# A matmul kernel with a planned order: one stored pair fewer, a finer table of bandwidth shares in the planner, and another layout of the scratch tiles in DRAM

## The chip, the cores and the metric

One core of one Trainium2 chip runs one launch of the kernel. The time is the device time of that launch in microseconds (us); smaller is better. The kernel before was run three times; the median counts.

## The reference

```python
def reference(a, b, bias):          # a, b: 4096 x 4096 float32, bias: 4096
    return np.tanh(np.matmul(a, b) + bias)
```

## The kernel before

**Two levels of Strassen.** The kernel computes the product in fp16 (all loads from `a` and `b` cast from float32 on their way in) with fewer multiplications than the plain method. Rows go in *pairs* of 2 x 128 rows, sixteen in all (`NP`), and two pairs form a *duo* (eight duos). Columns go in four blocks of 1024 (`c` = 0 to 3). For a pair, A is a 2 x 2 matrix of tiles: a11, a12, a21, a22, each 128 rows by 2048 of the inner dimension, 4 KB per partition in fp16. The seven products P1 to P7 need four of these or their sums s1 to s4. At the second level (`fine_left`, `fine_right`, `Fine`) two pairs together are split once more: a product of two pairs is made from seven products of half tiles with 256 columns instead of eight. So most matmuls of the program are 128x256 (line 798), the rest 128x512 (lines 783 and 1560).

**The stages.** *The opening* (lines 1456 to 1663) computes column block 0 for the row blocks 0 to 7, which are the pairs 0 to 3, with plain matmuls while the first data arrives. Then, still for c = 0, `run_duo` takes the duos 2 to 7 in turn. Their A is read from the input in natural order (`natural_tile`, line 504: four DMAs by 32 partitions on POOL's queue, and two DVE transposes, line 476, per tile of 1 MB of float32), the sums are formed on DVE, and the four tiles a11, a12, a22, s2 (`BASIS`) of each pair are written to DRAM scratch (`keep`, line 550), so that the later column blocks can fetch them without a transpose. For c = 1, 2, 3 the kernel runs `pass_one` (products P1 and P2, and P6 for c = 2, 3) over all duos, and `pass_two` (P7, P6, P5, P4, P3) over all duos in reverse order. B's block of 1024 columns is read raw for each c (`raw_b`, line 717: sixteen tiles of 1 MB on POOL's queue); its sums are formed on DVE.

**What is stored, and when.** `FIRST = (0,)` (line 42) makes pair 0, one of the four pairs of the opening, a stored pair: at the end of the opening, lines 1656 to 1660 form s1 and s2 of pair 0 on DVE and write a11, a12, a22, s2 (512 KB each) to scratch on SP's queue. Pairs 1, 2 and 3 aren't stored; when c = 1 first needs them, `upper` (line 1229) reads a11 and a12 from the input once more, by natural tiles, and stores them, and later, in `pass_two`, `others` (line 1239) does so for a21 and a22, forms the sums and stores a22, s2 and s1, s3, s4. For a stored pair these two functions only fetch from scratch. With `ORDER[1] = (7, 6, 5, 0, 4, 1, 3, 2)` duo 0 (pairs 0 and 1) is the fourth duo of `pass_one` for c = 1, and the fifth of `pass_two`.

**The scratch in DRAM.** Each name of each duo has one DRAM tile of five half tiles (line 421, `[P, 5, TP, P]`; a half tile is 2 KB per partition, 256 KB in all). All five halves of a partition lie side by side, so a partition's row is 10 KB, and a transfer of two neighbouring halves (`move`, line 538, on SP's queue) is 128 pieces of 4 KB; a transfer of one half is 128 pieces of 2 KB. The traffic with scratch is most of what SP's queue carries; the rest of it are the output tiles (256 KB each, pieces of 2 KB), the partial sums `state` (512 KB, pieces of 4 KB) and the bias.

**What sets the order.** No order is written out by hand across engines. All work is recorded as operations with an engine, an estimated duration, an emitter, reads and writes (`Plan.add`, line 150), ranked by due time (`rank`), and placed by a list scheduler (`schedule`, line 218) that plays the program through with its own durations. The order in which it starts the operations is the order of the instructions on each engine; nothing else of it reaches the chip. Two DMA queues are played: POOL's (all loads from `a` and `b`) and SP's (everything else), each with at most `RING = 8` DMAs under way. When both carry something, `rates` (line 277) deals the bandwidth: SP's transfer gets 0.64 if it is a load into SBUF and 0.47 if it is a store (`SHARE`, line 51), POOL gets the rest. A load is only placed when a buffer of the 51 `PLACES` is free.

Of the kernel before, what the change touches and what calls it, by code (L numbers as in the profile page):

```python
# [10 lines left out]
P = 128  # L11
# [6 lines left out]
TP = T // 2  # L18
# [3 lines left out]
fp16 = mybir.dt.float16  # L22
# [16 lines left out]
THREE = (False, False, True, True)  # L39
LATER = 6  # L40
HOLD = (1, 1, 1, 1)
FIRST = (0,)
WHOLE = ()
SPARE = ("a11", "a12", "a22")
AHEAD = (("s1", "s3", "s4"), ("s1", "s3", "s4"), ("s1", "s3", "s4"), ("s1", "s3", "s4"), (), ())
# [2 lines left out]
SMALL = 5  # L48
RING = 8
DMA = {"POOL": (384e3, 3.65), "LATER": (384e3, 5.0), "in": (399e3, 3.86), "out": (369e3, 3.5)}  # L50
SHARE = (0.64, 0.47)
RISE = ((), (4, 4, 4, 4, 4, 4, 4, 4), (4, 4, 4, 4, 4, 4, 4, 4), (4, 4, 4, 4, 4, 4, 4, 4))
SECONDS = (0, 8, 8, 8)
STEEP = ((0, 1, 1, 1, 1, 2), (), ())
# [73 lines left out]
class Op:  # L128
    __slots__ = (
        "parts", "n", "eng", "dur", "lag", "emit", "preds", "succs", "bufs", "nbytes", "hw", "soft", "early", "lead", "reach", "far",  # L130
        "unsent", "flying", "flow", "wait",
        "due", "left", "start", "done", "ready",
    )

# [1 line left out]
class Plan:  # L136
# [10 lines left out]
        self.bufs.append(buf)  # L147
        return buf

    def add(self, eng, dur, emit, reads=(), writes=(), nbytes=0, hw=True, soft=None, early=0.0, lead=0.0, reach=1e9, after=None):  # L150
        early, far = early if isinstance(early, tuple) else (early, self.FAR)
        op = Op()
        op.n, op.eng, op.dur, op.emit = len(self.ops), eng, dur, emit
        op.nbytes, op.hw, op.soft, op.early, op.lead = nbytes, hw, soft, early, lead
        op.parts = 4 if dur > 1 and not hw else 1
        op.reach, op.far = reach, far
        if nbytes:
            kind = "LATER" if not hw and early else "POOL" if not hw else "out" if soft is not None else "in"
            op.flow, op.wait = nbytes / DMA[kind][0], DMA[kind][1]
        op.lag = op.wait + op.flow if nbytes else self.LATE  # L160
        preds, seen = set(), {}
        for group, writing in ((reads, False), (writes, True)):
            for access in group:
                buf, atoms = access if isinstance(access, tuple) else (access, access.atoms)
                if isinstance(buf, Bank):
                    if eng == "PE":
                        preds |= buf.rest
                        buf.rest = set()
                        buf.pe = op
                        buf.writer, buf.readers = {}, {}  # L170
                        continue
                    if buf.pe:
                        preds.add(buf.pe)
                    buf.rest.add(op)
                else:
                    seen[buf] = True
                for i in atoms:
                    if i in buf.writer:
                        preds.add(buf.writer[i])
                    if writing:  # L180
                        preds.update(buf.readers.get(i, ()))
                        buf.writer[i], buf.readers[i] = op, []
                    else:
                        buf.readers.setdefault(i, []).append(op)
        if after:
            preds.add(after)
        preds.discard(op)
        op.bufs = [b for b in seen if b.cls]
        for b in op.bufs:
            b.users += 1  # L190
        if eng == "PE":
            if self.last_pe:
                preds.add(self.last_pe)
            self.last_pe = op
        op.preds = preds
        op.succs = []
        for p in sorted(preds, key=lambda p: p.n):
            p.succs.append(op)
        self.ops.append(op)
        return op  # L200
# [17 lines left out]
    def schedule(self):  # L218
# [9 lines left out]
        pipes = {e: [] for e in ready}  # L228
# [47 lines left out]

        def rates():

            live = [(e, p) for e, p in pipes.items() if p]
            if len(live) == 1:  # L280
                return [(live[0][1], 1.0)]
            part = {p[0][1].eng: SHARE[p[0][1].soft is not None or not p[0][1].bufs] for _, p in live if p[0][1].hw}
            return [(p, 1 - sum(part.values()) if e == "POOL" else part[e]) for e, p in live]

        def flow(now):
            shares = rates() if any(pipes.values()) else []
            for p, r in shares:
                p[0][0] -= (now - clock[0]) * r
            clock[0] = now
            ended = False  # L290
            for p, _ in shares:
                while p and p[0][0] < 1e-6:
                    op = p.pop(0)[1]
                    op.done = now + op.wait
                    heapq.heappush(events, (op.done, op.n, 1))
                    ended = True
            return ended

        def next_flow(now):
            if any(pipes.values()):  # L300
                clock[1] += 1
                at = now + min(max(p[0][0], 1e-6) / r for p, r in rates())
                heapq.heappush(events, (at, clock[1], 3))

        while events:
            now = events[0][0]
            while events and events[0][0] <= now + 1e-9:
                _, n, kind = heapq.heappop(events)
# [3 lines left out]
                elif kind == 4:  # L312
                    op = self.ops[n]
# [3 lines left out]
                elif kind == 1:  # L317
                    op = self.ops[n]
# [16 lines left out]
                elif kind == 2:  # L335
                    op = self.ops[n]
                    insort(ready[op.eng], (op.due, op.n))
            for eng, waiting in ready.items():
# [5 lines left out]
                for i, (_, n) in enumerate(waiting):  # L344
                    op = self.ops[n]
# [34 lines left out]
def kernel(  # L380
# [18 lines left out]
    dram = ctx.enter_context(tc.tile_pool(name="dram", bufs=1, space=bass.MemoryType.DRAM))  # L399
    ctx.enter_context(tc.manual_schedule())  # L400

    plan = Plan()
    add, new = plan.add, plan.buf

    def fixed(name, shape, dtype):
# [12 lines left out]
    for i in range(NP // 2):  # L418
        for name in STORED:
            buf = scratch[name, i] = Buf(f"{name}_{i}", None, cls=None, atoms=5)  # L420
            buf.tile = dram.tile([P, 5, TP, P], fp16, name=f"{name}_{i}")

    states = []
    for i in range(NP // 2):
        buf = Buf(f"state_{i}", None, cls=None)
# [11 lines left out]
    def dve(n, emit, reads, writes, wide=False, **kw):  # L437
        add("DVE", 0.08 + n / (960 if wide else 1900), emit, reads, writes, **kw)

    def act(n, emit, reads, writes, **kw):  # L440
        add("ACT", 0.09 + n / 1200, emit, reads, writes, **kw)
# [11 lines left out]
    ALL = slice(None)  # L453
# [8 lines left out]
    def finish(src, row, col):  # L462

        o = new("o", [P, NB], fp32, "out")
        act(NB, lambda: nc.scalar.activation(o[ALL], src[ALL], TANH), (src,), (o,), soft=2.0)
        store(o, row, col, NB)
# [27 lines left out]
    def load_rows(tl, srcs, nbytes):  # L494


        def emit():
            for q in Q_ORDER:
                src, key = srcs(q)
                nc.gpsimd.dma_start(out=tl[(ds(q * QP, QP), *key)], in_=src)  # L500

        add("POOL", 4 * 0.55, emit, (), (tl,), nbytes=nbytes, hw=False)

    def natural_tile(pair, name, s, soft=None):

        r, h = int(name[1]) - 1, int(name[2]) - 1
        tl = new("nat", [P, 4, T * QP])
        s[name] = new(name, [P, T, P], atoms=2)

        def srcs(q):  # L510
            src = a[ds((2 * pair + r) * P, P), ds(q * KQ + h * T * QP, T * QP)]
            return src.rearrange("(mb p) k -> p mb k", p=QP), ()

        load_rows(tl, srcs, P * T * P * 4)
        for u in range(2):

            def emit(dst=s[name], tl=tl, u=u):
                transpose(dst, tl[ALL, ds(2 * u, 2), ALL], 0, u * 2 * QP)

            add("DVE", turn_time(1024), emit, (tl,), ((s[name], (u,)),), soft=soft)  # L520
# [17 lines left out]
    def move(name, duo, first, tl, t0, n, out, **kw):  # L538

        box = scratch[name, duo]  # L540
        dram_, key = (box, range(first, first + n)), (ALL, ds(t0 * TP, n * TP))
        sb = tl if out else (tl, range(t0, t0 + n))

        def emit():
            far, near = box[ALL, ds(first, n)], tl[key].rearrange("p (n t) m -> p n t m", n=n)
            nc.sync.dma_start(out=far if out else near, in_=near if out else far)

        add("SP", 0.34, emit, (sb if out else dram_,), (dram_ if out else sb,), nbytes=P * n * TP * P * 2, **kw)
# [906 lines left out]

    early = set(range(4, NP)) | set(FIRST)

# [9 lines left out]
    def mb(m, j):  # L1467
        return banks[2 * (m % 4) + j]
# [14 lines left out]
    first = new("first", [P, 4, 4, TB * QP], atoms=4)  # L1483
# [169 lines left out]
    for m, j in swapped:  # L1653
        down(m, j, T, 2 * T, stop=True)
        finish(mb(m, j), m, j * NB)
    for p in FIRST:
        s = {f"a{r + 1}{h + 1}": aq[2 * p + r, h] for r in range(2) for h in range(2)}
# [114 lines left out]
```

## Time and profile before

| | |
|---|---|
| median of 3 runs | 1464.31 us (1462.56 to 1467.89) |
| the profiled execution | 1466.24 us, of which 1464.5 us are the span from first to last instruction |
| mean granted TensorE clock | 0.997 |
| busy in the span | PE 1444.2 us, DVE 1112.8, ACT 461.3, POOL 304.3 |
| SP's DMA queue (q1) | 318.29 MB, 62.1% of the 16 DMA engines' span |
| POOL's DMA queue (q0) | 73.44 MB written, 31.4% |
| HBM, read and written | 324.01 MB and 141.03 MB |

PE is the matmul engine, DVE the vector engine, ACT the scalar engine, POOL the engine that issues the loads from the inputs, SP the one that issues all other DMAs. A row of the grouped views has: line, engine, operation, out<-in, count, then busy time and mean duration of one. A row of the timeline has: start, duration, engine, line, operation, count, and in brackets how long the engine sat idle before it and who ended that wait. A row of the DMA view has: queue, packets, MB, share of the 16 engines' time in the stretch asked for; MB of q0 are counted as written, after the cast, which is half of what is read. A queue's packets are the pieces of its transfers and, for about one in nine, a semaphore write of 4 bytes.

### The profile page before, as it was taken

The page shows a single profiled execution, that of the slowest core. Times are in us where ns is not written, and L with a number is a line of the kernel's source. Part 1 is how long each engine was busy: PE and PEld are TensorE (multiplying, and loading weights), DVE is VectorE, ACT ScalarE, POOL GpSimd, SP SyncE. Part 2 cuts the span into 40 slices and gives each one's busy share as a digit, 9 for nine tenths or more (in the row PEclk, how much of TensorE's full clock was granted, in tenths as well). Part 3 has the DMA queues.
Part 4 walks back from the last instruction along what each step waited for, and adds up shares of the span by engine and source line. Part 5 has one row for each costly group of instructions (what it writes and reads, how often), then busy time and mean ns, then how long its engine had stood idle before and what let it go on. Part 6 is the DMA issues. An engine that isn't in the chain of part 4 may idle for free.

```text
span 1464.5 us, 28902 instructions
## 1 busy us (share of the span) xinstructions
PE 1444.2 (99%) x11256; PEld 1101.4 (75%) x11256; DVE 1112.8 (76%) x1739; ACT 461.3 (31%) x1062; POOL 304.3 (21%) x565
## 2 busy tenths in 40 slices
PE   9998999999999999999999999999999999999998
PEld 4444445554578887778878888888888888888887
DVE  3558877776967997785697799977679588986765
ACT  2111111121233332433333332334343332243433
POOL 8754334324333201100130300000210220000000
PEclk9999999999999999999999999999999999999999
DMA  9999999999999979977999988688999897777772
GB/s 175 198 244 293 268 273 288 307 279 272 250 302 316 297 236 281 334 264 287 307 296 348 284 258 288 228 267 272 259 307 340 220 264 267 243 262 270 250 267 89
DMA packets 199754, 393.58 MB, mean 269 GB/s; under 512 B 26048, under 2 KB 92096, under 8 KB 199616
## 3 DMA queue, kind: packets, MB, share of 16 engines
q1 hardware_dynamic: 116928, 318.29, 62.1%
q0 software_dynamic: 82688, 73.44, 31.4%
q8 instruction: 88, 1.44, 0.4%
q14 instruction: 50, 0.41, 0.1%
HBM read 324.01 MB, written 141.03 MB: 318 GB/s over the span
## 4 chain that ended last, share of the span: by engine, by line
PE 74%; DMA 11%; DVE 3%; issue 1%; POOL 1%; ACT 0%; SPq 0%; DVEq 0%; POOLq 0%
PE ps L798 57%; PE ps L783 18%; DMA b<-in_b_dram 6%; DMA nat<-in_a_dram 3%; DMA a<-a 1%; DVE parts L444 1%; DMA bias<-in_bias_dram 0%; DMA out_dram<-parts 0%; DVE ps L444 0%; DVE zs L636 0%; POOL nat L500 0%; DMA out_dram<-p 0%; DMA ys<-s 0%; DVE a L476 0%; DVE s L444 0%
## 5 line engine op out<-in xcount | busy, mean ns | idle before, releaser
L710 POOL DMA_DIRECT2D b<-in_b_dram x256 | 137.6, 541 | 576.9 <-DMA out_dram<-st 197.4
L447 ACT COPY ps<-ps 128x256 f32<-128x256 f32 (+1 forms) x290 | 106.1, 366 | 351.0 <-PE ps L798 334.8
L500 POOL DMA_DIRECT2D nat<-in_a_dram x240 | 129.6, 543 | 300.5 <-DMA nat<-in_a_dram 78.9
L798 PEld LDWEIGHTS <-zs 128*128 128x128 f16 x1424 | 139.3, 98 | 18.6 <-issue 0.7
L798 PEld LDWEIGHTS <-ys 128*128 128x128 f16 x1360 | 133.1, 98 | 15.4
L783 PEld LDWEIGHTS <-s 128*128 128x128 f16 x752 | 74.2, 99 | 90.2 <-issue 8.9
L798 PEld LDWEIGHTS <-ya 128*128 128x128 f16 x1296 | 126.8, 98 | 16.0
L798 PEld LDWEIGHTS <-za 128*128 128x128 f16 x1232 | 120.5, 98 | 14.2 <-issue 0.2
L798 PEld LDWEIGHTS <-xs 128*128 128x128 f16 x1184 | 115.8, 98 | 17.8 <-issue 2.2
L447 ACT COPY parts<-ps 128x256 f32<-128x256 f32 (+1 forms) x185 | 71.6, 388 | 182.9 <-DVE ps L444 83.5
L783 PE MATMUL ps<-t,s 128*128 128x512 f16 x528 | 121.1, 385 | 4.5 <-DVE ps L444 4.5
L798 PEld LDWEIGHTS <-parts 128*128 128x128 f16 x1104 | 108.0, 98 | 12.5
L476 DVE STREAM_TRANSPOSE a<-nat 128x512 uint32<-128x512 uint32 x120 | 78.7, 691 | 50.2 <-DMA nat<-in_a_dram 39.2
L1560 PE MATMUL ps<-b,o 128*128 128x512 f16 x512 | 111.4, 379 | 0.7 <-DVE ps L1585 0.6
L444 DVE TENSOR_TENSOR parts<-ps,parts 128x256 f32<-128x256 f32 (+1 forms) x173 | 75.9, 439 | 47.4 <-PE ps L798 39.3
L798 PEld LDWEIGHTS <-xa 128*128 128x128 f16 x1024 | 100.2, 98 | 14.6 <-issue 2.7
L783 PEld LDWEIGHTS <-a 128*128 128x128 f16 x592 | 57.9, 98 | 67.7
L444 DVE TENSOR_TENSOR ps<-ps,parts 128x256 f32<-128x256 f32 (+1 forms) x189 | 83.8, 445 | 24.6 <-PE ps L798 15.7
L636 DVE TENSOR_TENSOR zs<-xs,ys 128x2048 f16<-128x2048 f16 x74 | 90.1, 1218 | 15.4 <-PE ps L798 11.5
L798 PE MATMUL ps<-b,zs 128*128 128x256 f16 x784 | 101.6, 273 | 0.0
L1560 PEld LDWEIGHTS <-o 128*128 128x128 f16 x512 | 49.8, 98 | 60.9 <-issue 1.0
L636 DVE TENSOR_TENSOR za<-xa,ya 128x2048 f16<-128x2048 f16 x60 | 73.1, 1218 | 17.0 <-DMA out_dram<-cs 10.5
(140 smaller groups left out, 2533.9 us busy)
## 6 DMA issues: line engine op xcount, KB each, us to landing
ys<-s SPq DMA_DIRECT2D x74, 512.0 KB, 5.0
xs<-s SPq DMA_DIRECT2D x74, 512.0 KB, 5.3
b<-in_b_dram POOLq DMA_DIRECT2D x256, 128.0 KB, 8.5
ya<-a SPq DMA_DIRECT2D x64, 512.0 KB, 6.4
xa<-a SPq DMA_DIRECT2D x64, 512.0 KB, 6.7
nat<-in_a_dram POOLq DMA_DIRECT2D x240, 128.0 KB, 9.1
out_dram<-parts SPq DMA_DIRECT2D x112, 256.0 KB, 6.1
a<-a SPq DMA_DIRECT2D x32, 512.0 KB, 7.5
```

The costliest lines, as they stand in the source:

```text
L444: dve(n, lambda: nc.vector.tensor_tensor(out=o(), in0=x(), in1=y(), op=op), reads, writes, wide, **kw)
L447: act(n, lambda: nc.scalar.copy(o(), x()), reads, writes, **kw)
L476: nc.vector.transpose(dst[ALL].rearrange("P t m -> P (t m)").bitcast(pair32).rearrange("P (U m) -> P U m", m=P)[:, ds(t0 // 2, nu), ds(row ...
L500: nc.gpsimd.dma_start(out=tl[(ds(q * QP, QP), *key)], in_=src)
L636: nc.vector.tensor_tensor(out=halves(z), in0=halves(x), in1=halves(y)[:, ds(0, 1)].broadcast_to([P, 2, TP * P]), op=SUB,)
L710: nc.gpsimd.dma_start(out=dst.rearrange("p t j n -> p t (j n)") if j is None else dst, in_=src)
L783: nc.tensor.matmul(bank[ALL], left_tile(left, k + t + shift), rb.tile(t), start=start and k == t0 and t == 0, stop=k + t == t0 + nt - 1, s ...
L798: nc.tensor.matmul(bank[ALL, HALF[half]], left_tile(buf, at_ * TP + i * TB + t), rb.tile(t), start=False, stop=i == 1 and t == TB - 1, ski ...
L1560: nc.tensor.matmul(bank[ALL], left_tile(left, t), rb.tile(tb), start=start, stop=stop, skip_group_check=True,)
```

## The change

Three edits. `FIRST` becomes empty: no pair of the opening is stored, and pair 0 is treated as pairs 1 to 3 are. The scratch tile becomes `[5, P, TP, P]`: each half tile is one block of 256 KB, with 2 KB per partition, and a transfer of two halves is 256 pieces of 2 KB. The planner's two shares become a table of 2 x 3, which deals POOL's share by what the two queues carry at their heads: POOL's B tiles (0) or A tiles (1), against SP's loads (0), stores to the output (1) or stores to scratch (2).

```diff
-FIRST = (0,)
+FIRST = ()
...
-SHARE = (0.64, 0.47)
+SHARE = ((0.35, 0.51, 0.53), (0.44, 0.47, 0.15))
...
-    def add(self, eng, dur, emit, reads=(), writes=(), nbytes=0, hw=True, soft=None, early=0.0, lead=0.0, reach=1e9, after=None):
+    def add(self, eng, dur, emit, reads=(), writes=(), nbytes=0, hw=True, soft=None, early=0.0, lead=0.0, reach=1e9, after=None, rows=False):
...
+            op.kind = int(rows) if not hw else 0 if soft is None else 2 if writes else 1
...
         def rates():
 
-            live = [(e, p) for e, p in pipes.items() if p]
+            live = [p for p in pipes.values() if p]
             if len(live) == 1:
-                return [(live[0][1], 1.0)]
-            part = {p[0][1].eng: SHARE[p[0][1].soft is not None or not p[0][1].bufs] for _, p in live if p[0][1].hw}
-            return [(p, 1 - sum(part.values()) if e == "POOL" else part[e]) for e, p in live]
+                return [(live[0], 1.0)]
+            soft_, hard = pipes["POOL"], pipes["SP"]
+            part = SHARE[soft_[0][1].kind][hard[0][1].kind]
+            return [(soft_, part), (hard, 1 - part)]
...
-            buf.tile = dram.tile([P, 5, TP, P], fp16, name=f"{name}_{i}")
+            buf.tile = dram.tile([5, P, TP, P], fp16, name=f"{name}_{i}")
...
     def load_rows(tl, srcs, nbytes):
...
-        add("POOL", 4 * 0.55, emit, (), (tl,), nbytes=nbytes, hw=False)
+        add("POOL", 4 * 0.55, emit, (), (tl,), nbytes=nbytes, hw=False, rows=True)
...
     def move(name, duo, first, tl, t0, n, out, **kw):
...
         def emit():
-            far, near = box[ALL, ds(first, n)], tl[key].rearrange("p (n t) m -> p n t m", n=n)
+            far, near = box[ds(first, n)].rearrange("n p t m -> p n t m"), tl[key].rearrange("p (n t) m -> p n t m", n=n)
             nc.sync.dma_start(out=far if out else near, in_=near if out else far)
```

In the changed program PE has the same 11256 matmuls of the same shapes. Storing pair 0 takes two DVE sums and four stores of 512 KB out of the opening. For c = 1 it adds four natural tiles of A (sixteen DMAs on POOL and eight DVE transposes) and four stores of 512 KB, and takes out four fetches of 512 KB; one DVE sum more stands there. The order on DVE, ACT, POOL and SP changes, above all in the opening, for c = 0 and for c = 1; the order on PE is the same.

More of the change, by code (lines that the diff above doesn't have):

```diff
@@ L130 @@
         "parts", "n", "eng", "dur", "lag", "emit", "preds", "succs", "bufs", "nbytes", "hw", "soft", "early", "lead", "reach", "far",
-        "unsent", "flying", "flow", "wait",
+        "unsent", "flying", "flow", "wait", "kind",
         "due", "left", "start", "done", "ready",
```

## Prediction

> **What bounds the kernel now.** I read the page first, then PE's waits, then the timeline at each wait, then the DMA view in chosen stretches.
>
> ```profile
> span 1464.5 us, 28902 instructions
> PE 1444.2 (99%) x11256; PEld 1101.4 (75%) x11256; DVE 1112.8 (76%) x1739; ACT 461.3 (31%) x1062; POOL 304.3 (21%) x565
> L476 DVE STREAM_TRANSPOSE a<-nat 128x512 uint32<-128x512 uint32 x120 | 78.7, 691 | 50.2 <-DMA nat<-in_a_dram 39.2
> L500 POOL DMA_DIRECT2D nat<-in_a_dram x240 | 129.6, 543 | 300.5 <-DMA nat<-in_a_dram 78.9
> PE ps L798 <- DVE ps L444: 8.4, 11, 1.7
> PE ps L783 <- DVE ps L444: 4.5, 1, 4.5
> ```
>
> PE is busy in all but 20.3 us, and the change takes no matmul away. So a gain can only come out of PE's gaps, and the last two rows say nearly all there is: 13 us in twelve waits for DVE. Losses have no such limit. The longest gap stands in the opening:
>
> ```profile
> 145.87 0.71 DVE L476 STREAM_TRANSPOSE a<-nat 128x512 uint32<-128x512 uint32 x1 [1.21 <-DMA nat<-in_a_dram]
> 146.50 0.67 DVE L444 TENSOR_TENSOR ps<-ps,bias 128x512 f32<-128x512 f32 x1
> 147.22 3.14 PE L783 MATMUL ps<-t,s 128*128 128x512 f16 x7 [4.45 <-DVE ps L444]
> 147.22 27.04 PE ps L783 x112
> 197.70 24.41 PE ps L783 x112
> 125.00:150.00 25.00, 20.55 (x90) 8.91 (x89) 23.49 (x34) 2.42 (x5) 9.44 (x19) 0.92 1.13 300
> 475.00:500.00 25.00, 23.26 (x214) 20.68 (x213) 21.67 (x34) 7.97 (x21) 8.12 (x15) 1.00 1.14 293
> ```
>
> DVE takes its work in order. A transpose stood ahead of the small sum that PE needed, and waited for a late tile of A; DVE itself was ready. PE lost 4.45 us, and then more: the 112 matmuls behind the gap took 27.04 us, 112 like them elsewhere 24.41, so 2.63 us went to the lower clock (0.92 granted in that window). The other gaps:
>
> ```profile
> 471.89 1.03 PE L798 MATMUL ps<-f4b,a 128*128 128x256 f16 x8 [0.81 <-DVE ps L444]
> 479.90 1.03 PE L798 MATMUL ps<-f4b,a 128*128 128x256 f16 x8 [1.74 <-DVE ps L444]
> 627.12 1.03 PE L798 MATMUL ps<-t,zs 128*128 128x256 f16 x8 [0.57 <-DVE ps L444]
> 637.47 1.03 PE L798 MATMUL ps<-f4t,xa 128*128 128x256 f16 x8 [0.44 <-DVE ps L444]
> 763.98 1.03 PE L798 MATMUL ps<-f4t,xa 128*128 128x256 f16 x8 [0.48 <-DVE ps L444]
> 783.28 1.03 PE L798 MATMUL ps<-f4b,a 128*128 128x256 f16 x8 [0.81 <-DVE ps L444]
> 791.29 1.03 PE L798 MATMUL ps<-f4b,a 128*128 128x256 f16 x8 [1.73 <-DVE ps L444]
> 1103.82 1.03 PE L798 MATMUL ps<-f4t,xs 128*128 128x256 f16 x8 [0.37 <-DVE ps L444]
> ```
>
> They stand where POOL reads B and A at the start of c = 1 (2.55 us), at duo 0's second visit (1.01), where B is read for c = 2 (3.02) and for c = 3 (0.37). In most of them DVE stood in front of a POOL tile that came late, as in the opening.
>
> **What POOL's tiles wait for.** The DMA view of two stretches in which POOL streams, the first beside SP's pieces of mostly 4 KB, the second beside pieces of 2 KB:
>
> ```profile
> q1 hardware_dynamic: 2985, 8.14, 65.8%
> q0 software_dynamic: 2843, 2.58, 45.1%
> ...
> q0 software_dynamic: 3472, 3.16, 63.1%
> q1 hardware_dynamic: 2560, 5.38, 51.5%
> ```
>
> The first two rows are of 752 to 786 us, the others of 105 to 135. Mean size of an SP packet: 8.14 MB / 2985 = 2.7 KB against 2.1 KB. POOL wrote 2.58 / 34 = 0.076 MB per us, then 3.16 / 30 = 0.105; a POOL tile is 0.524 MB as written, so it passes in 6.9 us beside large pieces and in 5.0 us beside small ones. SP falls from 0.239 to 0.179 MB per us. The packets are nearly one to one in the first case and 1.36 to 1 in the second: the queues seem to take turns by the piece. And a piece costs what its bytes cost: 65.8% x 16 x 34 / 8.14 = 44.0 us of one engine per MB, against 51.5% x 16 x 30 / 5.38 = 46.0. So halving SP's pieces costs the DMA engines 0 to 5% of SP's time, and hands bandwidth to POOL while both queues are full. I take the cost as 0: of the long stretches only the first 500 us have no DMA time to spare.
>
> **The change part by part.**
>
> *1. The opening without pair 0's store.* Rows of SP's queue and of DVE:
>
> ```profile
> 89.61 0.32 SPq L546 DMA_DIRECT2D a<-o  x1
> 92.61 0.33 SPq L546 DMA_DIRECT2D s<-s  x1
> 94.49 0.80 SPq L546 DMA_DIRECT2D a<-o  x1
> 107.43 1.31 DVE L476 STREAM_TRANSPOSE a<-nat 128x512 uint32<-128x512 uint32 x2 [2.93 <-DMA nat<-in_a_dram]
> ```
>
> Three of the four stores fall where POOL begins the natural tiles that are late from there on (DVE already waits 2.93 us for the first). Each is 0.524 MB x 44.0 / 16 = 1.44 us of all engines; three are 4.3 us, by which every tile behind them comes earlier. The two sums fall away beside that wait: nothing. The gap needs 4.45 us; the changed order helps further, as it puts 14 transposes ahead of the sum that stalled, not 15. I take 6.9 of 4.45 + 2.63 = 7.08 us as gained. Ends: 0, if other tiles are late instead, and 7.1.
>
> The trace shows a gap of 1.74 us that leaves the clock at 1.00 and one of 4.45 that lowers it, and nothing between. [...]
>
> *2. Pair 0's natural tiles in c = 1, first visit.* Two tiles more (eight DMAs, four transposes of 0.69 us), two fetches less, two stores more on SP: equal bytes there. Windows with POOL's count in the last brackets:
>
> ```profile
> 425.00:450.00 25.00, 25.00 (x232) 22.40 (x230) 20.13 (x35) 9.54 (x23) 8.38 (x16) 1.00 1.12 311
> 450.00:475.00 25.00, 24.20 (x223) 21.54 (x221) 19.39 (x30) 9.39 (x22) 7.85 (x15) 1.00 1.11 317
> ```
>
> With the 15 of the window quoted above, that is 46 DMAs, 11.5 tiles, in 75 us: 6.5 us a tile. The start of c = 1 takes sixteen tiles of B and six of A now, eight then. At 6.5 us each the two more make the last ones 13 us late; at 5.0, 24 tiles take 120 us against 143, and the 2.55 us of gaps go too. Halfway between the two rates above, 5.95, 24 tiles take the same 143. I take that: 0, ends -2.6 and +13. It isn't the fast end, since free buffers pace POOL there too. The transposes and the sum lie in DVE's idle time (20 of 25 us busy).
>
> *3. The same at the second visit.* Now two tiles, then four:
>
> ```profile
> 611.41 4.28 POOL L500 DMA_DIRECT2D nat<-in_a_dram  x8 [50.04 <-ACT ps L447]
> 629.67 0.71 DVE L476 STREAM_TRANSPOSE a<-nat 128x512 uint32<-128x512 uint32 x1 [1.05 <-DMA nat<-in_a_dram]
> 544.03 2.17 POOL L500 DMA_DIRECT2D nat<-in_a_dram  x4 [48.80 <-PE ps L798]
> L476 DVE STREAM_TRANSPOSE a<-nat x8: 670/698/712, 562.9 to 570.4; 128x512 uint32<-128x512 uint32 x8
> ```
>
> The second tile's transpose ran 18.3 us after the first issue, just too late. Duo 1 already does what duo 0 will do: four tiles, the last transpose 26.4 us after the first issue, and no gap of PE. From 611.41 that is 637.8; the changed order needs the fourth tile 4.5 us of matmuls after the place where the second is needed now, so at 634.2: 3.6 late. At 5.0 us a tile, (18.3 - 2 x 1.9) + 2 x 5.0 = 24.5, it is 1.7 late; at 6.9, without that relief, 32.1 after issue, 9.3 late, with 1.01 of gaps there already. I take 2 us of gaps where now are 1.01: +1, ends -1 and +8.
>
> *4. B's tiles for c = 2 and c = 3.* At 5.0 instead of 6.9 us a tile even the first comes 1.9 us earlier, more than the longest gap (1.73): -3.0 for c = 2. For c = 3 I take 0, since SP's loads are tight there (below). Ends -3.4 and 0 without the relief.
>
> *5. The planner's table* changes orders only, which parts 1 to 4 count as they stand. SP's issue of 256 pieces isn't in the trace; 128 take 0.32 us. Ends 0 and another 0.32 each, hidden behind SP's waits except in bursts of eight: 2.6 us once. I take 0.
>
> Sum: -6.9 + 0 + 1 - 3.0 = -8.9. The profiled execution took 1466.24 us (span 1464.5 and 1.74 around it), so 1457.3; the median of the runs, 1464.31, is 1.93 lower, so **1455.4**.
>
> **The rivals.**
>
> *SP becomes late.* What POOL gains SP loses (0.239 to 0.179). The tightest place is the start of c = 3:
>
> ```profile
> q1 hardware_dynamic: 1708, 5.69, 76.5%
> DMA to landing us min/median/max: 11.7/12.7/14.3
> 1098.24 0.33 SPq L546 DMA_DIRECT2D xa<-a  x1
> ```
>
> SP alone moves 5.69 MB in 1096 to 1116 there, and a load issued at 1098 lands some 13 us later. Eight such loads, 4.2 MB, take 17.5 us at the one rate and 23.4 at the other: +5.9. Against it: POOL has two tiles there, not a stream. With part 2's and 4's gains gone as well (+3) the time is 1464.
>
> *Turns go by bytes, so POOL gains nothing* (the other side). Then the large and small pieces differ only because SP was often empty from 105 to 135. Part 1 stays at -6.9, part 2 gives up to +13 less the margin of some tiles, say +9, part 3 +8, part 4 0: +10, **1474**. It decides from a tile interval of 6.2 us in the start of c = 1 on (24 x 6.2 - 143 = 6, which eats part 1). For it: the 6.5 us there now. Against it: the packet counts. [...]
>
> *The pieces cost more than their bytes*, since scratch loads of 2 KB are in no row: at 5% of SP's engine time in the first 500 us, some 12 us of 250, +12, with part 1 kept: 1469.
>
> **How the numbers follow.** Chances: forecast 0.5 (its own range 1450 to 1461), SP late 0.2, turns by bytes 0.18, dear pieces 0.12. Some 0.5%, 7.3 us, is about what a measurement of this kernel can tell from no change. Faster by more means under 1457: 0.36 of the forecast's half and 0.04 of SP late, 0.40. Slower means over 1471.6: 0.12 of turns by bytes, 0.05 of dear pieces and 0.01 of SP late, 0.18. Within: 0.42. The range 1450 to 1473 leaves out some 0.05 below and 0.12 above.
>
> **What would show it.** Part 1: no gap near 142 to 147 and a clock of 1.00. The turns: q0 near 0.1 MB per us wherever B is read. Part 2: gaps between 410 and 500. Part 3: gaps between 615 and 640. SP late: PE's gaps from 1095 to 1120 grow, with loads that land after over 14 us. I am wrong if new gaps arise for c = 0, where I expect none.

## The result and the profile after

| | before | after |
|---|---|---|
| median | 1464.54 us (6 runs, 1462.56 to 1467.89) | 1475.38 us (6 runs, 1470.20 to 1478.59) |
| ratio to before, 95% interval | | 1.0066 [1.0051, 1.0081] |
| the profiled execution, its span | 1466.24, 1464.5 us | 1475.63, 1473.9 us |
| span less busy time of PE | 20.3 us | 27.4 us |

The change makes the kernel 0.66% slower, 10.8 us between the medians; the prediction said 1455.4 us, and 1450 to 1473 as its range. The head of the changed kernel's page and its DMA queues (packets, MB, share of the 16 engines):

```profile
span 1473.9 us, 28996 instructions
PE 1446.5 (98%) x11256; PEld 1101.5 (75%) x11256; DVE 1117.9 (76%) x1746; ACT 460.6 (31%) x1062; POOL 313.6 (21%) x581
q1 hardware_dynamic: 161664, 316.20, 61.7%
q0 software_dynamic: 84992, 75.53, 32.5%
```

The same matmuls take 2.3 us more (1446.5 against 1444.2), and PE idles 7.1 us more (27.4 against 20.3): together the 9.4 us by which the spans differ. SP's queue has 161664 packets where it had 116928, for 2 MB less, and takes no more of the engines (61.7% against 62.1%). PE's waits after (total, times, longest):

```profile
PE ps L800 <- DVE ps L446: 10.1, 10, 1.8
PE ps L785 <- DVE ps L446: 5.1, 1, 5.1
PE ps L785 <- DVE a L446: 4.3, 1, 4.3
```

(Line numbers are two higher than before.) The opening's single wait of 4.5 is still there, with 5.1, and a second of that size has come. The timeline of PE after; the second and third rows are undisturbed groups of 32 and of 16 such matmuls:

```profile
149.24 8.75 PE L785 MATMUL ps<-t,s 128*128 128x512 f16 x32 [5.11 <-DVE ps L446]
157.83 7.07 PE L785 MATMUL ps<-b,a 128*128 128x512 f16 x32
164.74 3.62 PE L785 MATMUL ps<-b,s 128*128 128x512 f16 x16
...
192.56 5.86 PE L785 MATMUL ps<-b,a 128*128 128x512 f16 x16 [4.28 <-DVE a L446]
```

And the windows of those stretches (PE, weight loads, DVE, ACT, POOL; then granted clock, DMA share, GB/s):

```profile
150.00:175.00 25.00, 25.00 (x111) 11.11 (x110) 21.85 (x39) 3.55 (x6) 6.45 (x12) 0.94 1.05 280
175.00:200.00 25.00, 20.72 (x115) 11.43 (x113) 15.57 (x24) 5.58 (x11) 10.80 (x20) 0.86 1.11 262
```

Both gaps are followed by a lower clock: 8.75 instead of 7.07 us for 32 matmuls, 5.86 instead of 3.62 for 16. The gap at 192 us and its lower clock, 4.28 + 2.24 = 6.5 us, are most of the 9.4 us that the span lost.

**What DVE waits for has changed.** DVE's waits between 105 and 400 us, before and then after:

```profile
DVE a L476 <- DMA nat<-in_a_dram: 35.8, 16, 6.0
```

```profile
DVE a L478 <- DMA nat<-in_a_dram: 13.0, 6, 7.2
DVE s L446 <- DMA out_dram<-parts: 12.5, 3, 5.7
DVE parts L446 <- DMA out_dram<-parts: 8.9, 6, 2.9
DVE s L446 <- DMA a<-parts: 7.9, 2, 6.1
DVE parts L446 <- DMA s<-parts: 4.7, 3, 1.9
```

Before, DVE waited 35.8 us for POOL's tiles and never for a store. After, it waits 13.0 for tiles and, with three smaller rows, 38.5 us for *stores of SP*: it wants to write into a buffer that a store is still reading. Of these 38.5 us, 23.7 end with a store to the output (`out_dram<-parts`), the rest with a store to scratch. Such waits stand ahead of the first gap, and are links in the chain to the second. DVE's timeline after, then POOL's:

```profile
120.88 1.23 DVE L446 TENSOR_TENSOR s<-a,a 128x2048 f16<-128x2048 f16 x1 [6.09 <-DMA a<-parts]
137.49 1.23 DVE L446 TENSOR_TENSOR s<-a,a 128x2048 f16<-128x2048 f16 x1 [2.07 <-DMA out_dram<-parts]
148.50 0.69 DVE L446 TENSOR_TENSOR ps<-ps,bias 128x512 f32<-128x512 f32 x1
188.63 1.30 DVE L478 STREAM_TRANSPOSE a<-nat 128x512 uint32<-128x512 uint32 x2 [7.25 <-DMA nat<-in_a_dram]
```

```profile
152.42 4.30 POOL L502 DMA_DIRECT2D nat<-in_a_dram  x8 [8.94 <-DVE a L478]
164.35 2.15 POOL L502 DMA_DIRECT2D nat<-in_a_dram  x4 [7.63 <-DMA out_dram<-parts]
178.12 4.30 POOL L502 DMA_DIRECT2D nat<-in_a_dram  x8 [11.62 <-PE ps L800]
```

The sum for which PE waits until 149.24 runs at 148.50 in a DVE that is busy ahead of it and had stood 6.09 + 2.07 = 8.2 us behind two stores. So DVE is late; that frees the buffers of the natural tiles late, and POOL idles 8.94 us behind DVE and 7.63 behind another store. From 143 to 177 us it issues 13 DMAs, where before it was 19:

```profile
nat<-in_a_dram POOLq DMA_DIRECT2D x19, 128.0 KB, 7.3
```

```profile
nat<-in_a_dram POOLq DMA_DIRECT2D x13, 128.0 KB, 6.6
```

Then the tile that DVE transposes at 188.63, issued from 178.12 on, comes too late, and PE stands until 192.56. The last link there isn't a store: by the profile PE ended POOL's wait of 11.62 us, and PE had itself lost 5.11 us, and run at a lower clock, shortly before. (The kernel before has a wait of POOL for PE of 16.0 us between 140 and 195 us, without a gap.) So for the second gap it is argued, not shown by these rows, that the stores began it.

The last number of each of the two DMA rows is the median time to landing: POOL's transfers land *sooner* than before (6.6 against 7.3). POOL's queue isn't slow; it is asked too late. SP's stores did get slower there: from 143 to 177 us the stores of 512 KB of a took 7.5 us (4.9 before) and the half tiles `s<-parts` 8.9 (4.3), two or three of each.

### The profile page after: what moved, and what is told of

Read it like the earlier page. It is cut to its first block, busy times and chain, and to the rows that moved or that the text cites. A ratio compares the mean times of both kernels' runs of the same rounds, so it can differ in the third digit from the quotient of the medians.

```text
span 1473.9 us, 28996 instructions
## 1 busy us (share of the span) xinstructions
PE 1446.5 (98%) x11256; PEld 1101.5 (75%) x11256; DVE 1117.9 (76%) x1746; ACT 460.6 (31%) x1062; POOL 313.6 (21%) x581
## 3 DMA queue, kind: packets, MB, share of 16 engines
q1 hardware_dynamic: 161664, 316.20, 61.7%
## 5 line engine op out<-in xcount | busy, mean ns | idle before, releaser
L502 POOL DMA_DIRECT2D nat<-in_a_dram x256 | 138.5, 545 | 318.2 <-DMA nat<-in_a_dram 51.1
L785 PE MATMUL ps<-t,s 128*128 128x512 f16 x512 | 116.3, 383 | 5.4 <-DVE ps L446 5.1
L800 PEld LDWEIGHTS <-parts 128*128 128x128 f16 x1104 | 108.0, 98 | 12.5
L478 DVE STREAM_TRANSPOSE a<-nat 128x512 uint32<-128x512 uint32 x128 | 83.7, 690 | 22.4 <-DMA nat<-in_a_dram 13.4
```

Of the source, the lines that this page charges most:

```text
L478: nc.vector.transpose(dst[ALL].rearrange("P t m -> P (t m)").bitcast(pair32).rearrange("P (U m) -> P U m", m=P)[:, ds(t0 // 2, nu), ds(row ...
L785: nc.tensor.matmul(bank[ALL], left_tile(left, k + t + shift), rb.tile(t), start=start and k == t0 and t == 0, stop=k + t == t0 + nt - 1, s ...
L800: nc.tensor.matmul(bank[ALL, HALF[half]], left_tile(buf, at_ * TP + i * TB + t), rb.tile(t), start=False, stop=i == 1 and t == TB - 1, ski ...
```

## The experiments

The ratio is to runs of the kernel before on the same chip. "Play" is the planner's own run through the program, with its own durations; its medians and those of the chip are over the transfers from 105 to 340 us, from issue to landing.

| kernel | median us | ratio to before |
|---|---|---|
| e1 first edit alone | 1461.91 | 0.9981 [0.9970, 0.9992] |
| e2 layout alone | 1462.36 | 0.9979 [0.9969, 0.9990] |
| e3 table alone | 1466.59 | 1.0016 [1.0006, 1.0027] |
| e4 first edit and layout | 1462.32 | 0.9981 [0.9967, 0.9994] |
| e5 layout and table | 1479.00 | 1.0101 [1.0086, 1.0115] |
| e6 first edit and table | 1466.84 | 1.0017 [1.0004, 1.0031] |
| all three edits (after) | 1475.38 | 1.0066 [1.0051, 1.0081] |
| e7 after, with 0.53 for 0.15 | 1461.86 | 0.9980 [0.9967, 0.9993] |
| e8 after, with only 0.15 new | 1479.17 | 1.0112 [1.0091, 1.0133] |
| e9 after, stores fast alone | 1478.53 | 1.0085 [1.0062, 1.0109] |
| e10 after, tiles slow alone | 1474.89 | 1.0063 [1.0043, 1.0084] |
| e11 after, with 0.40 for 0.15 | 1459.52 | 0.9953 [0.9933, 0.9974] |
| e12 after, with 0.70 for 0.15 | 1466.99 | 1.0011 [0.9997, 1.0026] |
| e13 after, stores later in the play | 1465.91 | 1.0015 [1.0001, 1.0030] |
| e14 after, with 0.30 for 0.15 | 1471.13 | 1.0046 [1.0028, 1.0064] |
| e15 e11, pair 0 stored | 1463.64 | 0.9995 [0.9982, 1.0008] |
| e16 e11, old layout | 1459.46 | 0.9968 [0.9953, 0.9982] |

### Which edit: e1 to e6

The edits are those of the change, one by one and in pairs:

```diff
-FIRST = (0,)
+FIRST = ()
```

> The kernel before with the first edit alone: no stored pair in the opening; old scratch layout, old shares. Three theories of why the whole change is 0.66% slower (+11 us in the profiled execution). PLANNER (mine): the new table of shares puts the instructions of DVE, ACT and POOL for c = 0 into an order that has gaps of PE near 149 and 192 us (5.1 and 4.3 us, and some 2.7 us of lower clock behind each); then this kernel loses the opening's gap (up to -7.1 us) and pays up to +6 us in c = 1 for 6.5 us tiles: 1458 to 1470, with no gap over 3 us near 192 us. QUEUE: the pieces of 2 KB make SP's transfers late and with them the buffers; then this kernel too is at 1458 to 1470. PAIR 0: its four natural tiles in c = 1 cost more than the opening gives; then it is slower by 5 us or more, with PE's new gaps between 410 and 500 us and none new before 400.

```diff
-            buf.tile = dram.tile([P, 5, TP, P], fp16, name=f"{name}_{i}")
+            buf.tile = dram.tile([5, P, TP, P], fp16, name=f"{name}_{i}")
...
-            far, near = box[ALL, ds(first, n)], tl[key].rearrange("p (n t) m -> p n t m", n=n)
+            far, near = box[ds(first, n)].rearrange("n p t m -> p n t m"), tl[key].rearrange("p (n t) m -> p n t m", n=n)
```

> The kernel before with the second edit alone: scratch tiles by halves, so that transfers of two halves are 256 pieces of 2 KB. The order of every engine's instructions is that of the kernel before, so only the queues' turns differ. PLANNER: POOL's tiles come at about 5 us instead of 6.9 us; the gaps of PE behind late POOL tiles (2.6 us in c = 1, 3.0 in c = 2, the opening's 4.5 and its 2.6 of lower clock in part) shrink: -3 to -12 us, 1452 to 1461. QUEUE: SP's loads and stores are late, PE has new gaps at c = 0 near 150 and 190 us behind buffers that an SP store frees: +5 to +11 us, 1470 to 1477. PAIR 0: as PLANNER.

```diff
-SHARE = (0.64, 0.47)
+SHARE = ((0.35, 0.51, 0.53), (0.44, 0.47, 0.15))
```

(with `kind`, `rows` and the new `rates`)

> The kernel before with the third edit alone: the planner's new table of shares, which changes orders only; old stored pair, old layout. PLANNER: the order is worse wherever POOL and SP stream together, with gaps of over 3 us for c = 0, and POOL's tiles still take 6.5 to 6.9 us: +5 to +15 us, 1469 to 1480. QUEUE and PAIR 0: within 4 us of the kernel before.

> The changed kernel with the old shares in the planner (no stored pair in the opening, layout by halves). PLANNER: what was forecast for the whole change holds here: 1452 to 1461, no gap over 3 us near 149 or 192 us. QUEUE: as slow as the changed kernel, 1470 to 1478. PAIR 0: 1468 to 1478, with the loss between 410 and 500 us.

The first two edits gain about 0.2% each, and no more together; that is 2 to 3 us, less than I had summed. QUEUE falls with e2 and PAIR 0 with e1: neither is slower. The table alone costs little (1.0016): 1466.59 us is below PLANNER's 1469 to 1480 and within the 4 us of the others, though the gaps behind DVE for c = 0 that PLANNER foretold are there, 3.6 and 3.3 us. So the loss must lie in a combination with the table:

> The changed kernel with pair 0 still stored in the opening (old FIRST), so layout and new shares together. Alone they gave 0.9979 and 1.0016, so without an interaction 1464 us. ENTRY (now mine): of the new table only one number is far from the old shares, POOL's 0.15 for an A tile beside a store to scratch (before 0.53); the planner thinks that such stores get 0.85 of the bandwidth and frees their buffers too early in its play; on the chip POOL and DVE then wait for buffers that SP's stores hold, and the more so with pieces of 2 KB, which slow SP: 1468 to 1478, with waits of POOL of over 5 us between 140 and 195 us that end with a store or an engine, and PE gaps of over 3 us there. CHANCE (rival): every new order has its own two or three unlucky places, and the table as such is no worse: 1458 to 1466 here.

> The changed kernel with the old layout (first edit and new shares). Without an interaction 1463.5 us. ENTRY: SP's transfers of 512 KB keep pieces of 4 KB and more of the bandwidth, so the stores come nearer to what the planner thinks: 1463 to 1470, with less wait for buffers of stores than in the changed kernel, but gaps of PE of over 3 us at 140 to 195 us. CHANCE: 1458 to 1478, nothing follows.

Table and layout together are as slow as the whole change, or slower; table and first edit are not. Layout and table don't add up: -0.2% and +0.2% make +1.0%. e3 and e5 have the same order on every engine. In e5 the stores of 512 KB of s take longer from issue to landing, here e3 and then e5 from 105 to 335 us:

```profile
s<-s SPq DMA_DIRECT2D x14, 512.0 KB, 6.9
```

```profile
s<-s SPq DMA_DIRECT2D x14, 512.0 KB, 7.7
```

and DVE's waits for stores from 105 to 400 us grow from 30.4 to 40.6 us in all. e6 and the whole change also share one order, and there DVE's waits for stores do not differ (38.7 and 38.5 us), although ENTRY said less of them for e6; what differs is POOL's waits for stores from 140 to 195 us (6.5 against 11.6 us) and PE's second gap (2.2 against 4.3). e5, 1479.00 us, lies 1 us above ENTRY's range, e6 within it.

### Which number: e7 and e8

```diff
-SHARE = ((0.35, 0.51, 0.53), (0.44, 0.47, 0.15))
+SHARE = ((0.35, 0.51, 0.53), (0.44, 0.47, 0.53))
```

> The changed kernel with one number of the table set back: POOL's share for an A tile beside a store to scratch 0.53 instead of 0.15; the other five stay. ENTRY: the loss goes, 1456 to 1464, and POOL's waits between 140 and 195 us for buffers shrink from some 32 us in all to under 20. CHANCE or the other entries of the table: 1468 to 1478 as the changed kernel.

```diff
-SHARE = ((0.35, 0.51, 0.53), (0.44, 0.47, 0.15))
+SHARE = ((0.36, 0.53, 0.53), (0.36, 0.53, 0.15))
```

> The changed kernel with the old shares in all entries but one: only the 0.15 for an A tile beside a store to scratch is kept. ENTRY: 1470 to 1478, gaps of PE of over 3 us between 140 and 195 us. CHANCE or the other entries: 1458 to 1466.

Both came out as ENTRY said, e8 1 us above its range: without the 0.15 the loss is gone (0.9980), with the 0.15 alone it is there in full (1.0112). CHANCE falls as it was worded; that some of a single kernel's time is the luck of its order isn't excluded by that (e10, below). In e7, DVE's waits from 105 to 400 us have the form that they had before, for tiles and hardly for stores:

```profile
DVE a L478 <- DMA nat<-in_a_dram: 40.8, 21, 4.5
DVE a L478 <- DMA a<-parts: 0.9, 1, 0.9
```

Its window of the opening, and that of the kernel before:

```profile
100.00:150.00 50.00, 49.80 (x231) 22.53 (x230) 44.83 (x69) 8.48 (x15) 21.61 (x40) 1.00 1.15 281
```

```profile
100.00:150.00 50.00, 45.55 (x206) 20.27 (x204) 40.62 (x60) 6.59 (x12) 19.00 (x36) 0.96 1.14 293
```

PE is busy 49.80 of 50 us at full clock, against 45.55 at 0.96: here part 1 of the prediction holds.

### Which effect of the number: e9 to e14

With 0.15, two estimates of the play move at once: stores to scratch are fast, A's tiles are slow. A third follows from them: the play lets SP's transfers pass one after another, so a store to the output that stands behind one to scratch is done sooner too. Its median there is 5.5 us with 0.15 and 10.5 with 0.53; on the chip it is 6.4 and 7.7.

```diff
-            return [(soft_, part), (hard, 1 - part)]
+            slow = soft_[0][1].kind == 1 and hard[0][1].kind == 2
+            return [(soft_, 0.3 if slow else part), (hard, 0.85 if slow else 1 - part)]
```

> The 0.15 did two things to the planner's play at once: stores to scratch get 0.85 and A's tiles 0.15. Medians from issue to landing, 105 to 340 us: in the changed kernel's play a store takes 5.5 us and on the chip 6.8, a tile 15.3 and 10.7; with 0.53 in that place a store takes 13.4 and 10.2, a tile 14.2 and 14.2. Here the two are taken apart: beside each other the store keeps 0.85, but the tile is given 0.30 (the two no longer add up to 1), so that in the play a store takes 5.5 us and a tile 12.5. STORES (mine): a plan that thinks stores faster than the chip's reuses their buffers too early, and DVE and POOL, which work in order, wait for them: 1469 to 1480. TILES: the loss comes from thinking the tiles slow, which puts transposes late and so frees their buffers late: 1457 to 1465 here.

The same two lines with 0.45 and 0.47:

> The other half: beside each other the store gets 0.47 as before and the tile 0.45, so that in the play a store takes 13.6 us (not too fast) and a tile 16.5 (slower than on the chip). STORES: 1458 to 1468. TILES: 1469 to 1480.

Then the number itself, as 0.40 and 0.70:

> The changed kernel with 0.40 in place of 0.15 (in the play a store takes 7.2 us and a tile 14.7). STORES: 7.2 is still less than the 10.2 that stores take on the chip when both queues are kept full, so part of the loss stays: 1462 to 1472. TILES: a tile is as in the kernel with 0.53 (14.7 against 14.2), so 1458 to 1464.

> The changed kernel with 0.70 in place of 0.15 (in the play a store takes 13.4 us and a tile 10.7, faster than on the chip with full queues, 14.2). STORES: stores aren't thought too fast, so no loss from buffers: 1457 to 1466, with at most small gaps behind late tiles. TILES: also no loss from late transposes: 1457 to 1466. If instead any wrong share costs, tiles now come later than planned and the opening's gap of 4 us and its lower clock come back: 1466 to 1474.

e9 is as slow as STORES said, and its rows show the mechanism bare; DVE and then PE:

```profile
152.43 0.69 DVE L447 TENSOR_TENSOR parts<-a 128x1024 f16<-128x1024 f16 x1 [6.74 <-DMA s<-parts]
```

```profile
154.99 5.44 PE L786 MATMUL ps<-t,s 128*128 128x512 f16 x16 [6.74 <-DVE ps L447]
```

DVE stands 6.74 us behind a store to scratch, and PE 6.74 us behind DVE. But e10 is slow too, against STORES, and as slow as TILES said. Its gaps are elsewhere, none from 100 to 270 us, and no wait for a store stands directly ahead of the two long ones; DVE isn't idle ahead of them, but busy with other work:

```profile
375.49 1.89 PE L801 MATMUL ps<-b,a 128*128 128x256 f16 x8 [4.49 <-DVE a L447]
524.64 1.01 PE L801 MATMUL ps<-b,xs 128*128 128x256 f16 x4 [5.83 <-DVE b L447]
```

There the two shares add up to 0.92, so its play is slow as a whole; what made these gaps wasn't followed further. e11 missed the number of STORES and fits that of TILES: it has the lowest ratio of all. e12, 1466.99 us, lies above the 1466 of both and in the range given for the case that any wrong share costs. It shows the opposite error: in its play a tile takes 10.7 us and is trusted, and the opening's old gap is back, behind a DVE that waits for a tile:

```profile
141.57 1.31 DVE L478 STREAM_TRANSPOSE a<-nat 128x512 uint32<-128x512 uint32 x2 [2.34 <-DMA nat<-in_a_dram]
```

```profile
150.31 9.24 PE L785 MATMUL ps<-t,s 128*128 128x512 f16 x32 [5.32 <-DVE ps L446]
```

Two more kernels take the effects apart in the changed kernel. One keeps 0.15 and lets stores land later in the play; the other puts 0.30, at which the play's tiles are as with 0.40 and only its stores are faster.

```diff
-DMA = {"POOL": (384e3, 3.65), "LATER": (384e3, 5.0), "in": (399e3, 3.86), "out": (369e3, 3.5)}
+DMA = {"POOL": (384e3, 3.65), "LATER": (384e3, 5.0), "in": (399e3, 3.86), "out": (369e3, 6.0)}
```

> The changed kernel with its 0.15, and one other number of the planner: the fixed part of a store's time, 3.5 us, is set to 6.0 (for all stores), so that in the play a store to scratch takes 8.0 us instead of 5.5, which is more than the 6.8 that it takes on the chip; a tile stays at 14.6. STORES: 1458 to 1467, no gap of PE over 3 us between 140 and 195 us. TILES: 1470 to 1478, the gaps near 149 and 192 us stay.

> The changed kernel with 0.30 in place of 0.15. In the play a tile takes 14.7 us, exactly as with 0.40, and a store 5.9 us against 7.2 with 0.40 and 5.5 with 0.15. STORES: nearly as slow as with 0.15, 1468 to 1477. TILES: as fast as with 0.40, 1457 to 1463.

STORES gave the number of both, TILES of neither. e14, with tiles as in e11, is at 1.0046. In e13 PE's gaps at 149 and 192 us are gone, although the 0.15 stands; its windows, and its one wait of PE from 100 to 400 us:

```profile
100.00:150.00 50.00, 50.00 (x234) 22.68 (x232) 42.05 (x64) 7.36 (x13) 21.24 (x39) 1.00 1.15 281
150.00:200.00 50.00, 47.65 (x250) 24.23 (x249) 43.63 (x70) 9.36 (x18) 18.46 (x34) 1.00 1.13 298
```

```profile
PE ps L800 <- ACT ps L449: 2.3, 1, 2.3
```

So with longer stores in the play the gaps go; *all* stores were made longer, so e13 doesn't tell those to scratch from those to the output. After c = 0 the kernel gives part of this back (from 400 to 600 us PE is busy 192.06 us, in e7 196.87); the reason wasn't followed. The sizes side by side ("store" is a store to scratch):

| kernel | store: play, chip (us) | tile: play, chip (us) | median us |
|---|---|---|---|
| after (0.15) | 5.5, 6.8 | 14.9, 10.7 | 1475.4 |
| e14 (0.30) | 5.9, 7.6 | 14.7, 11.6 | 1471.1 |
| e11 (0.40) | 7.2, 8.9 | 14.7, 12.8 | 1459.5 |
| e7 (0.53) | 13.4, 10.2 | 14.2, 14.2 | 1461.9 |
| e12 (0.70) | 13.4, 8.3 | 10.7, 10.8 | 1467.0 |
| e13 (0.15, stores +2.5) | 8.0, 8.4 | 14.6, 12.5 | 1465.9 |

The chip's times follow the order too: the two fastest kernels of this table, e7 and e11, have the *longest* transfers (stores 10.2 and 8.9 us, tiles 14.2 and 12.8; their DMA moved 286 and 289 GB/s from 105 to 177 us, the changed kernel's 278). That e11 beats e7 doesn't follow from STORES, since its stores, too, are thought 1.7 us faster than they are; DVE waits 28 us for stores there, at places where PE has something else to do. Nor does the size of the error, or the sum of the waits, put the kernels in order: stores are thought 1.3 us too fast in the changed kernel, 1.7 in e14 and 1.7 in e11, and DVE waits 26 us for stores in e14 and 25 in e13. What costs is a wait with PE standing behind it, and where those fall is settled anew by each order.

### Whether the gain of 0.40 needs the other edits: e15 and e16

> The kernel with 0.40, but pair 0 stored in the opening (old FIRST). If the first edit carries part of the gain of 0.9953 against the kernel before, this one is slower than the one with 0.40 alone by the opening's store, some 2 to 6 us: 1461 to 1466. If it carries nothing: 1458 to 1461.

> The kernel with 0.40, but the old layout of the scratch tiles (pieces of 4 KB for two halves); the order of all engines is that of the kernel with 0.40. POOL's tiles take longer, SP's transfers less long. If halves help as they did alone (0.9979): 1461 to 1464. If, with stores thought fast, quicker stores are worth more, as with the full table (1466.8 against 1475.4): 1452 to 1459.

These are e11 with `FIRST = (0,)` and with `[P, 5, TP, P]` and its old `box[ALL, ds(first, n)]`. Stored, pair 0 costs 4 us by the medians and 6 by the ratios (0.9995 against 0.9953): the first edit is worth having. The old layout gives 0.9968, 1459.46 us, between the two ranges; the intervals overlap, so the layout by halves isn't shown to add anything once the number is right. e11 has the lowest ratio, and e16 can't be told from it; e1, e2, e4 and e7 are also faster than the kernel before, by about 0.2%.

## Why the prediction was wrong

**The step that failed is number 5**: "The planner's table changes orders only, which parts 1 to 4 count as they stand. ... I take 0." I compared where the transposes stand relative to the sum that PE awaits, and not what the new order assumes of the stores. Whatever is placed into a buffer must wait for the last reader of that buffer (DVE's 38.5 us for stores above), and with 0.15 the play let readers be done in 5.5 us that take 6.8 and more. After and e7 differ in that number alone; their ratios, 1.0066 and 0.9980, put the price at 0.86%, 12.6 us: more than the sum of the rest, with the other sign. This is the price beside the layout by halves: there the table costs 0.9 to 1.2% (after against e4, e5 against e2), beside the old layout 0.2 to 0.4% (e3 against before, e6 against e1). "Count as they stand" failed in this too: the sum had no term for what the table and the layout do together.

*Part 1, the opening (-6.9 us).* The gap didn't go but changed its cause: 5.11 us behind a DVE that stores had held up, instead of 4.45 behind one that a tile had held up. The mechanism was right where the 0.15 is not: e1 has 3.33 us there, e4 1.72 (with another of 3.24 at 180 us), e7 none over 0.5.

*The turns of the queues.* With the order of before and pieces of 2 KB (e2), SP's queue took 63.6% of the engines' time for the same 318.29 MB, against 62.1%: the cost of 0 was right within 2.4%. POOL's B and A tiles landed sooner from 425 to 500 us, before and then e2:

```profile
b<-in_b_dram POOLq DMA_DIRECT2D x32, 128.0 KB, 11.1
nat<-in_a_dram POOLq DMA_DIRECT2D x13, 128.0 KB, 13.0
```

```profile
b<-in_b_dram POOLq DMA_DIRECT2D x32, 128.0 KB, 9.0
nat<-in_a_dram POOLq DMA_DIRECT2D x12, 128.0 KB, 9.2
```

2.1 us for B; the 1.9 forecast were of the interval between tiles, not of the time to landing. That interval fell where B alone is read, from 6.6 us before (748 to 773 us) to 5.9 in e2 (745 to 768), about the middle rate that part 2 took, and the gaps of 3.0 us there are gone in e2. But from 425 to 500 us POOL wrote no more than before (6.42 against 6.52 MB), so the 0.1 MB per us named as a sign wasn't reached, and SP's loads landed later (`xa<-a` 14.4 against 9.5 us). From 105 to 335 us A's tiles landed later too (median 9.9 against 8.8 us) and SP's stores of a and s 1.5 to 1.9 later (8.9 against 7.4 and 8.7 against 6.8): there SP paid, and POOL didn't gain. The whole edit gave 0.2%, 3 us.

*Part 2 (0, ends -2.6 and +13).* PE's gaps from 410 to 500 us are 4.7 us against 2.6: +2, within the ends. *Part 3 (+1).* No wait of PE is left from 612 to 640 us: -1. *Part 4 (-3.0).* From 770 to 800 us 0.4 us of gaps stay: -2.6, right. New are 1.3 us at 836 and 1.4 at 1082, which I had no term for.

*The rivals.* "SP becomes late" came nearest, and for a reason it didn't name: not a load for which PE waits at c = 3, but a store that holds a buffer, in the opening and for c = 0. "The pieces cost more" is out, since layout alone is 3 us faster than before. "Turns go by bytes" fails where B alone is read (6.6 us a tile before, 5.9 in e2); from 105 to 335 us POOL gained nothing, as it said (20.54 MB before, 20.53 in e2). The remark that I would be wrong "if new gaps arise for c = 0" is what happened.

With the number set right, 1459.5 (e11) and 1461.9 (e7) lie within the forecast's own range of 1450 to 1461 or just above it: the sum of the other steps was 4 to 6.5 us too good.

What stays open: why e10 is slow, why 0.40 beats 0.53 (each number gives another order on four engines, and one order is one draw), how the second gap at 192 us begins, and whether buffers held by stores to the output or by stores to scratch matter more.

## What to carry to other kernels

A planner's bandwidth number isn't a harmless estimate: it decides which buffer is handed on when, and where a store is thought done too early, the engines stand behind it: in e9 DVE 6.74 us behind a store, and PE 6.74 us behind DVE. Before trusting such a number, lay the times that the plan gives each kind of transfer beside the times in the trace. Neither side of the error is safe: e10 and e12 have late stores in the play and are no faster than the kernel before, and the best one, e11, has them 1.7 us early. So run several values. When a profile shows short transfers and idle issuers (here 6.6 us for POOL's, and POOL idle for 8.94 and 7.63), look for who releases the buffers before you look at bandwidth.

## What the runs showed of the hardware

In these runs a gap of PE of some 3 us was followed by the lower clock in one place (3.24 us in e4) and not in another (3.33 us in e1); its length alone doesn't tell. The same 32 matmuls behind the opening's gap, in e16, e1 and e2:

```profile
146.52 7.13 PE L785 MATMUL ps<-t,s 128*128 128x512 f16 x32 [3.06 <-DVE ps L446]
```

```profile
146.66 7.20 PE L783 MATMUL ps<-t,s 128*128 128x512 f16 x32 [3.33 <-DVE ps L444]
```

```profile
146.63 8.75 PE L783 MATMUL ps<-t,s 128*128 128x512 f16 x32 [3.54 <-DVE ps L444]
```

Here gaps of up to 3.33 us leave the matmuls at 7.1 to 7.2 us; after 3.54 they take 8.75, 1.6 us more, for 0.2 us of gap. Other places of these runs don't agree with a bound between the two. In e15 matmuls of 128x256, of which eight take 1.04 us undisturbed, slow down within 1 us after a gap of 2.07 us (the next eight take 1.79). In e9 the 48 of 128x512 behind a gap of 3.25 us take as long as undisturbed (16 of them 3.62 us, 32 take 7.07), and 28 behind a gap of 2.68 us take more than 32 undisturbed:

```profile
420.94 1.03 PE L800 MATMUL ps<-f3b,za 128*128 128x256 f16 x8 [2.07 <-ACT parts L449]
421.81 1.79 PE L800 MATMUL ps<-f1b,ya 128*128 128x256 f16 x8
```

```profile
207.77 3.61 PE L786 MATMUL ps<-t,s 128*128 128x512 f16 x16 [3.25 <-DVE ps L447]
211.22 7.07 PE L786 MATMUL ps<-b,a 128*128 128x512 f16 x32
...
302.69 7.57 PE L786 MATMUL ps<-t,s 128*128 128x512 f16 x28 [2.68 <-DVE ps L447]
```

In e4 a gap of 3.24 us at 180 us was followed by a lower clock as well (0.93 granted from 165 to 190). So from 2.07 to 3.33 us these traces have both outcomes. Behind the longer gaps the matmuls were slow: 16 of 128x512 took 5.32 us after 3.88 (e14) and after 4.57 (e15), 5.86 after 4.28 (the changed kernel) and 5.44 after 6.74 (e9), against 3.62 undisturbed; 32 took 8.75 after 5.11 (the changed kernel) and 9.24 after 5.32 (e12), against 7.07.
